# Order of the TensorE products inside a split step and inside a differential head

## The chip, the cores and the metric

The kernel runs on one core of a Trainium2 chip. The metric is the device time of one execution in microseconds (us), the median of several executions; before the change it is 1139.26 us (three executions, 1139.25 to 1139.76).

## The reference, cut to what matters

One layer of a hybrid decoder on x of 256 tokens by 2048 columns, all in float32. One input projection of the normalised x (2048 columns wide) gives six blocks of 1024 columns; the first three feed eight differential heads, the last three eight stick-breaking heads. An output projection and a squared-ReLU MLP of 8192 hidden columns follow, each added to the residual, and a last RMSNorm.

```python
h = rmsnorm(x, ln1[l])
dq, dk, dv, sq, sk, sv = jnp.split(h @ w_in[l], split_points, axis=-1)
# differential head: two softmax maps over 64 dims each, values of 128 dims
w = probs(q1, k1) - lam * probs(q2, k2)
o = jnp.einsum("bhqk,bkhd->bqhd", w, v)
...
x = x + mixed @ w_out[l]
h = rmsnorm(x, ln2[l])
x = x + jnp.square(jax.nn.relu(h @ w_mlp_in[l])) @ w_mlp_out[l]
```

## The kernel before

**Numbers in two parts.** Every long product is made of three products of float32r operands. A matrix is split into H, its float32r rounding, and L, the rest; x.w is taken as xH.wH + xH.wL + xL.wH, summed in float32 in PSUM. The weights stream from HBM in chunks of 512 rows by 512 columns (1 MB, three buffers). ScalarE casts half a chunk to `wh` (L214) and VectorE subtracts to get `wl` (L217); such a half, 256 contraction rows by 512 columns, is a split step. Four pairs of `wh` and `wl` are in flight (six in the MLP), and the casts run three to five steps ahead of the products.

**Two forms of product.** `products_acc` (L248) keeps the activations in the array and moves the weights: three products of 512 columns for each contraction tile and token tile (L258 to L260). It serves dq, dk, dv, sv, the output projection (`oacc`) and the second MLP product (`ma`). `products_T` (L264) keeps the weights in the array and moves the activations. It serves sq and sk (`acc_sq`, `acc_sk`) and the first MLP product (`ia`). For one contraction tile and one tile of 128 weight columns it issues a long product, `wh` against H and L of the activations side by side (512 columns, L272), and a short one, `wl` against H alone (256 columns, L274), which is added to the second half of the same PSUM bank. A step of `products_T` has four column tiles times two contraction tiles, so eight long and eight short products. A group is the eight steps (2048 contraction rows) that fill four banks. In its last step each column tile is evacuated by `done(i)` as soon as its own products are out: ScalarE copies the second half of the bank, VectorE adds the first half to it (L568 for sq and sk).

**A differential head.** `diff_task` (L441) computes both score maps of a head into one tile `sc` of two PSUM banks, map m in bank m. A map has a 64-dim query and key: map 0 lies in partitions 0 to 63 of `qT` and `kT`, map 1 in partitions 64 to 127. For each map there is a mask product of 128 rows in bf16 (identity times mask, L451), a score product of query tile 1 against 256 keys (L453) and one of query tile 0 against 128 keys (L455). These two are plain float32, and the profile records each of them as two instructions. The attention tasks are generators that are advanced between the split steps; their instructions stand on the same TensorE queue as the products of the weight stream.

**Order.** Outside of the first seven steps, which are written out by hand, a scheduler with a timeline model of its own orders the instructions of an engine; it keeps to the program's order, except that it may put a ready instruction ahead of one that waits in its model.

Of the kernel before, what the change touches and what calls it, by code (L numbers as in the profile page):

```python
# [10 lines left out]
F32 = mybir.dt.float32  # L11
F32R = mybir.dt.float32r
BF16 = mybir.dt.bfloat16
# [3 lines left out]
PSUM = bass.MemoryType.PSUM  # L17

P = 128
S = 256  # L20
D = 2048
DFF = 4 * D
NT = S // P          # token tiles
KT = D // P          # contraction tiles of the model width
NB = 512             # columns of a weight block
CK = 4               # contraction tiles of one weight load
HK = 2               # contraction tiles of one split step
HG = 4               # heads of one column block
# [5 lines left out]
LN_IN = 2.0 ** -32                    # the Ln table ends at 2^64  # L34
LN_OUT = -16.0 * math.log(2.0)
LAM_INIT = 0.8 - 0.6 * math.exp(-0.3 * 0)
W_BUFS = 3           # weight loads in flight
S_BUFS = 4           # split steps in flight
START_ORDER = "x0 c0 x1 c1 m0 x2 c2 m1 c3 x3 m2 x4 c4 m3 c5 x5 m4 x6 c6 m5 c7 x7 m6"
WARM0, WARM1 = 5, 4  # products of zeros before and after the first transposes  # L40
AHEAD = 3            # split steps ahead of the products
# [3 lines left out]
def tile_hybrid_layer(  # L45
# [19 lines left out]
    """Every large product runs as three float32r passes: with x = H + L, H = float32r(x),  # L65
    x.w = xH.wH + xH.wL + xL.wH, all summed in float32 PSUM."""
# [9 lines left out]
    # ---------------------------------------------------------------- loads  # L76
# [16 lines left out]
    # ---------------------------------------------------------------- constants  # L93
# [14 lines left out]
    negtri = cpool.tile([P, P], F32, name="negtri")      # [l, j] = -1 where l >= j  # L108
# [5 lines left out]
    dmask = cpool.tile([P, 2 * P], BF16, name="dmask")   # [q, key]: key <= q is kept  # L114
    smask = cpool.tile([P, 2 * P], BF16, name="smask")   # [key, q]: key < q is kept
# [12 lines left out]
    # ---------------------------------------------------------------- helpers  # L128
    def rsqrt_mean(ss, n, width, name, r, eps=EPS, most=FMAX):
        """r = 1 / sqrt(ss / width + eps): exp(-ln/2), then one Newton step; 0 where the sum of  # L130
        squares exceeds `most` (it overflows, and the root of its inverse is 0)."""
        v = tiny.tile([P, n], F32, tag=f"v{n}", name=f"v_{name}")
        nc.vector.tensor_scalar(v, ss, 1.0 / width, eps, op0=ALU.mult, op1=ALU.add)
        nc.vector.tensor_scalar(v, v, TINY, BIG, op0=ALU.max, op1=ALU.min)
        lv = tiny.tile([P, n], F32, tag=f"lv{n}", name=f"lv_{name}")
        nc.scalar.activation(lv, v, AF.Ln, scale=LN_IN)
        r0 = tiny.tile([P, n], F32, tag=f"r0{n}", name=f"r0_{name}")
        nc.scalar.activation(r0, lv, AF.Exp, scale=-0.5, bias=lnout_c)
        a = tiny.tile([P, n], F32, tag=f"a{n}", name=f"a_{name}")
        nc.vector.scalar_tensor_tensor(a, v, -0.5, r0, op0=ALU.mult, op1=ALU.mult)  # L140
        nc.vector.tensor_tensor(a, a, r0, op=ALU.mult)
        nc.vector.scalar_tensor_tensor(a, a, 1.5, r0, op0=ALU.add, op1=ALU.mult)
        nc.vector.scalar_tensor_tensor(r, ss, most, a, op0=ALU.is_le, op1=ALU.mult)

    def split_pair(dst, ps, g, per_kt):
        """dst[:, kt, 0/1, :] = H / L of ps * g (g: one column per kt, or one for both)."""
        if per_kt:
            for j in range(HK):
                nc.scalar.activation(dst[:, j, 0, :], ps[:, j * S:(j + 1) * S], AF.Copy, scale=g[:, j:j + 1])
            for j in range(HK):  # L150
                nc.vector.scalar_tensor_tensor(dst[:, j, 1, :], ps[:, j * S:(j + 1) * S], g[:, j:j + 1],
                                               dst[:, j, 0, :].bitcast(F32),
                                               op0=ALU.mult, op1=ALU.subtract)
        else:
            pv = ps.rearrange("p (k s) -> p k s", k=HK)
            nc.scalar.activation(dst[:, :, 0, :], pv, AF.Copy, scale=g)
            nc.vector.scalar_tensor_tensor(dst[:, :, 1, :], pv, g,
                                           dst[:, :, 0, :].bitcast(F32),
                                           op0=ALU.mult, op1=ALU.subtract)

    # ---------------------------------------------------------------- weight stream
    jobs = []       # (chunk id, half, products, after)
    chunks = []     # weight views
# [10 lines left out]
    mlp = {"n": 0}  # pools of the second part  # L174
# [72 lines left out]
    # activations stationary, weights moving: acc[t] += act[:, tokens t].T @ w  # L247
# [15 lines left out]
    # weights stationary, activations moving: acc[i] = [wH.T @ xH | wH.T @ xL + wL.T @ xH]  # L263
    def products_T(get_acc, act, k0, done):  # L264
        def f(h, wh, wl):
            acc = get_acc()
            for i in range(NB // P):
                fs = slice(i * P, (i + 1) * P)
                for j in range(HK):
                    kt = k0 + h * HK + j  # L270
                    a = act(kt)
                    nc.tensor.matmul(acc[i], wh[:, j, fs], a.rearrange("p a s -> p (a s)"),  # L272
                                     start=kt == 0, stop=False, skip_group_check=True)
                    state["mm"] = nc.tensor.matmul(acc[i][:, S:2 * S], wl[:, j, fs], a[:, 0, :],  # L274
                                                   start=False, stop=kt == KT - 1, skip_group_check=True)
                if kt == KT - 1:
                    done(i)
        return f
# [17 lines left out]
    # ---------------------------------------------------------------- start: x -> xs  # L296
# [9 lines left out]
    def keep_clock_up(n, name):  # L306
        """products of zeros that nothing reads: the tensor engine's clock is halved until it
        has been busy for a while, and it has to wait for the first loads anyway."""
# [5 lines left out]
    lamc = cpool.tile([P, 2], F32, name="lamc")          # c, -lam * c with c = 1 / max(|lam|, 1)  # L314
    epsc = cpool.tile([P, 1], F32, name="epsc")          # eps * c^2
    mostc = cpool.tile([P, 1], F32, name="mostc")        # float32's largest value * c^2
# [72 lines left out]
    # ---------------------------------------------------------------- attention tasks  # L389
    grp = {}  # L390

    def prep_task(kind):
        """q / k of the differential heads: rotary, then heads transposed to [dim, token]."""
# [28 lines left out]
    def finish_pair(o, g, kt2, name, **norm):  # L422
        """per-head RMSNorm of o [q, (head, query tile), dim], transposed and split into mixT."""
# [17 lines left out]
    def diff_task(gi):  # L441
        while f"dk{gi}" not in grp:
            yield
        # outputs carry the factor c, so that their squares stay in range for any lam
        qT, kT, v = grp[f"dq{gi}"], grp[f"dk{gi}"], grp[f"dv{gi}", "src"]
        for h in range(HG):
            nm = f"d{gi}{h}"
            sc = ps_sc.tile([P, 2, 512], F32, tag="sc", name=f"sc_{nm}")
            for m in range(2):
                dm = slice(m * 64, (m + 1) * 64)  # L450
                nc.tensor.matmul(sc[:, m, P:3 * P], identb, dmask, start=True, stop=False,  # L451
                                 skip_group_check=True)
                nc.tensor.matmul(sc[:, m, 0:S], qT[dm, h, P:S], kT[dm, h, 0:S],  # L453
                                 start=False, stop=False, skip_group_check=True)
                nc.tensor.matmul(sc[:, m, S:S + P], qT[dm, h, 0:P], kT[dm, h, 0:P],  # L455
                                 start=False, stop=True, skip_group_check=True)
            yield
            nm4 = tiny.tile([P, 2, 2], F32, tag="nmax", name=f"nmax_{nm}")   # [query tile, map]
# [40 lines left out]
    def sb_task(gi):  # L499
        """scores as [key, query]: columns are (key tile 0, query tile 1), (0, 0), (1, 1)."""  # L500
# [47 lines left out]
    # ---------------------------------------------------------------- projections  # L548
# [3 lines left out]
    def proj_T_block(kind):  # L552
        """q / k of the stick-breaking heads, straight to [dim, token]."""
# [58 lines left out]
    # output projection: the first two column blocks stop before the last head group  # L612
# [50 lines left out]
    # ---------------------------------------------------------------- MLP stream  # L663
# [12 lines left out]
    FQ = 4                       # quarters of the hidden width  # L676
    FG = DFF // FQ // NB         # column groups of a quarter
# [34 lines left out]
    def out_group(q, nb):  # L712
# [29 lines left out]
        # the last column block: all of token tile 0, then token tile 1 in two column halves  # L742
# [55 lines left out]
    def square_base(t, n):  # L798
        """the sum over all but the last piece, ready before it."""
# [4 lines left out]
    def finish_tokens(t, base):  # L804
        """final RMSNorm of one token tile; all but the last column block are times ln_f already."""
# [38 lines left out]
    # ---------------------------------------------------------------- run  # L844
# [31 lines left out]
def _rope_table():  # L876
    """cos | cos and -sin | sin of the first 16 dims, [token in tile, token tile, 2, 16]."""
# [36 lines left out]
```

## Time and profile before

| | |
|---|---|
| median of three executions | 1139.26 us |
| span of the profiled execution, first to last instruction | 1137.4 us |
| what lies around the span (1139.26 less 1137.4) | 1.9 us |
| TensorE (PE) busy | 1126.2 us, 99% of the span |
| weight loads (PEld) | 948.9 us, 83% |
| VectorE (DVE) busy | 659.2 us, 58% |
| ScalarE (ACT) busy | 534.6 us, 47% |
| HBM traffic over the span | 182 GB/s |

The span is the profiled execution's own time inside the program; the sum of a change is made against it, and what lies around it is taken as constant. Ends of TensorE instructions in the records are modelled, so the time that a product costs is read from the start of one to the start of the next, not from its duration. PEld rows are the loads of the stationary operand; they run beside the products.

### The profile page before, as it was taken

The numbers are of one execution on the slowest core, as the hardware profiler recorded it, in microseconds if no ns is written. First come the engines' busy times: TensorE is split into PE (matmuls) and PEld (weight loads), VectorE is DVE, ScalarE is ACT, GpSimd is POOL, SyncE is SP. The second block draws the span as 40 slices with busy tenths as digits, with TensorE's granted clock in tenths as the row PEclk, the third lists the DMA queues.
The fourth block names the chain that finished last, engine by engine and source line by source line (L and its number), as shares of the span: only waits on it lengthen the run. The fifth ranks groups of instructions, "written<-read, shape, count | busy, mean of one in ns | idle before, by whom it ended". The sixth has DMA issues, their size and how long they took to land.

```text
span 1137.4 us, 14314 instructions
## 1 busy us (share of the span) xinstructions
PE 1126.2 (99%) x5725; PEld 948.9 (83%) x5725; DVE 659.2 (58%) x929; ACT 534.6 (47%) x761; POOL 2.9 (0%) x16
## 2 busy tenths in 40 slices
PE   9999999999999999999999999999999999999996
PEld 6887888888888888888888888888888888888886
DVE  5755656656655656565455556455655545565652
ACT  5644444555554644453334444334544333454531
POOL 1000000000000000000000000000000000000000
PEclk9999999999999999999999999999999999999998
DMA  8744454444555855555565555556555566555502
GB/s 289 231 153 157 148 179 146 149 148 148 184 187 199 322 182 185 185 186 193 197 199 186 186 185 185 192 194 196 189 192 185 185 190 191 191 190 195 193 35 74
DMA packets 105207, 207.68 MB, mean 183 GB/s; under 512 B 4114, under 2 KB 5172, under 8 KB 105012
## 3 DMA queue, kind: packets, MB, share of 16 engines
q1 hardware_dynamic: 104852, 206.24, 55.0%
q8 instruction: 45, 0.74, 0.3%
q10 hardware_dynamic: 288, 0.52, 0.1%
q14 instruction: 22, 0.18, 0.0%
HBM read 204.65 MB, written 2.10 MB: 182 GB/s over the span
## 4 chain that ended last, share of the span: by engine, by line
PE 97%; DMA 2%; SPq 1%; DVE 0%; ACT 0%; issue 0%; DVEq 0%; ACTq 0%
PE ia L272 21%; PE ia L274 11%; PE ma L260 10%; PE ma L259 10%; PE ma L258 10%; PE acc_sk L272 3%; PE acc_sq L272 3%; PE oacc L260 3%; PE oacc L258 3%; PE oacc L259 3%; PE acc_sq L274 1%; PE acc_sk L274 1%; PE acc_dk L258 1%; PE acc_dk L260 1%; PE acc_sv L258 1%; PE acc_dk L259 1%
## 5 line engine op out<-in xcount | busy, mean ns | idle before, releaser
L217 DVE TENSOR_TENSOR wl<-w,wh 128x1024 fp32r<-128x1024 f32 (+1 forms) x385 | 469.1, 1222 | 396.7 <-ACT wh L214 394.8
L214 ACT CAST wh<-w 128x1024 fp32r<-128x1024 f32 (+1 forms) x385 | 401.8, 1048 | 485.3 <-PE ma L260 189.7
L272 PE MATMUL ia<-xs,wh 128*128 128x512 f32 x1024 | 357.4, 393 | 0.0
L274 PE MATMUL ia<-xs,wl 128*128 128x256 f32 x1024 | 285.7, 281 | 0.0
L272 PEld LDWEIGHTS ia<-xs,wh 128*128 128x128 f32 x1024 | 191.1, 187 | 43.0
L274 PEld LDWEIGHTS ia<-xs,wl 128*128 128x128 f32 x1024 | 193.0, 189 | 1.2
L260 PE MATMUL ma<-wh,aT 128*128 128x512 f32 x480 | 187.9, 391 | 0.0
L259 PE MATMUL ma<-wl,aT 128*128 128x512 f32 x480 | 187.8, 391 | 0.0
L258 PE MATMUL ma<-wh,aT 128*128 128x512 f32 x480 | 187.7, 391 | 0.0
L258 PEld LDWEIGHTS ma<-wh,aT 128*128 128x128 f32 x480 | 90.1, 188 | 19.9
L259 PEld LDWEIGHTS ma<-wl,aT 128*128 128x128 f32 x480 | 90.1, 188 | 19.8
L260 PEld LDWEIGHTS ma<-wh,aT 128*128 128x128 f32 x480 | 90.1, 188 | 19.8
L258 PE MATMUL oacc<-wh,mixT 128*128 128x512 f32 x128 | 50.6, 395 | 0.0
L259 PE MATMUL oacc<-wl,mixT 128*128 128x512 f32 x128 | 50.2, 392 | 0.0
L260 PE MATMUL oacc<-wh,mixT 128*128 128x512 f32 x128 | 49.9, 394 | 0.0
L272 PE MATMUL acc_sq<-xs,wh 128*128 128x512 f32 x128 | 45.3, 396 | 0.0
L272 PE MATMUL acc_sk<-xs,wh 128*128 128x512 f32 x128 | 44.9, 398 | 0.0
L274 PE MATMUL acc_sq<-xs,wl 128*128 128x256 f32 x128 | 35.8, 284 | 0.0
L274 PE MATMUL acc_sk<-xs,wl 128*128 128x256 f32 x128 | 34.4, 283 | 0.0
L260 PEld LDWEIGHTS oacc<-wh,mixT 128*128 128x128 f32 x128 | 24.0, 188 | 5.0
L258 PEld LDWEIGHTS oacc<-wh,mixT 128*128 128x128 f32 x128 | 24.1, 188 | 4.9
L259 PEld LDWEIGHTS oacc<-wl,mixT 128*128 128x128 f32 x128 | 24.1, 188 | 4.9
(225 smaller groups left out, 1128.5 us busy)
## 6 DMA issues: line engine op xcount, KB each, us to landing
w<-in_w_mlp_in_dram SPq DMA_DIRECT2D x64, 1024.0 KB, 5.4
w<-in_w_mlp_out_dram SPq DMA_DIRECT2D x64, 1024.0 KB, 5.0
w<-in_w_in_dram SPq DMA_DIRECT2D x46, 1024.0 KB, 5.2
w<-in_w_out_dram SPq DMA_DIRECT2D x16, 1024.0 KB, 5.1
w<-in_w_in_dram SPq DMA_DIRECT2D x4, 512.0 KB, 7.7
x<-in_x_dram SPq DMA_DIRECT2D x3, 512.0 KB, 10.3
lnf_t<-in_ln_f_dram SPq DMA_DIRECT2D x1, 1024.0 KB, 6.5
out_dram<-x SPq DMA_DIRECT2D x4, 256.0 KB, 3.0
```

What stands on the lines that cost most here:

```text
L214: state["wh"] = nc.scalar.copy(wh[:, j], w[:, j])
L217: state["wl"] = nc.vector.tensor_tensor(wl[:, j], w[:, j], wh[:, j].bitcast(F32), op=ALU.subtract)
L258: nc.tensor.matmul(acc[t], a[:, 0, st], wh[:, j, :], start=s0, stop=False)
L259: nc.tensor.matmul(acc[t], a[:, 0, st], wl[:, j, :], start=False, stop=False)
L260: state["mm"] = nc.tensor.matmul(acc[t], a[:, 1, st], wh[:, j, :], start=False, stop=s1)
L272: nc.tensor.matmul(acc[i], wh[:, j, fs], a.rearrange("p a s -> p (a s)"), start=kt == 0, stop=False, skip_group_check=True)
L274: state["mm"] = nc.tensor.matmul(acc[i][:, S:2 * S], wl[:, j, fs], a[:, 0, :], start=False, stop=kt == KT - 1, skip_group_check=True)
```

## The change

There are two edits (the rest of the diff takes comments away).

In `products_T` the order of a step's 16 products changes. Before, long and short alternated for each column tile and contraction tile. Now all eight long products of a step come first and then its eight short ones. In the last step of a group, where each column tile is evacuated as soon as it is complete, the order is two long and two short for each column tile.

In `diff_task` the two mask products come first, then L453's product of map 0 and of map 1, then L455's product of map 0 and of map 1. Before, map 0 was completed before map 1 began. No product is added or left out by either edit.

```diff
     def products_T(get_acc, act, k0, done):
         def f(h, wh, wl):
             acc = get_acc()
-            for i in range(NB // P):
-                fs = slice(i * P, (i + 1) * P)
-                for j in range(HK):
-                    kt = k0 + h * HK + j
-                    a = act(kt)
-                    nc.tensor.matmul(acc[i], wh[:, j, fs], a.rearrange("p a s -> p (a s)"),
-                                     start=kt == 0, stop=False, skip_group_check=True)
-                    state["mm"] = nc.tensor.matmul(acc[i][:, S:2 * S], wl[:, j, fs], a[:, 0, :],
-                                                   start=False, stop=kt == KT - 1, skip_group_check=True)
-                if kt == KT - 1:
-                    done(i)
+            last = k0 + (h + 1) * HK == KT
+
+            def high(i, j):
+                kt = k0 + h * HK + j
+                nc.tensor.matmul(acc[i], wh[:, j, i * P:(i + 1) * P], act(kt).rearrange("p a s -> p (a s)"),
+                                 start=kt == 0, stop=False, skip_group_check=True)
+
+            def low(i, j):
+                kt = k0 + h * HK + j
+                state["mm"] = nc.tensor.matmul(acc[i][:, S:2 * S], wl[:, j, i * P:(i + 1) * P], act(kt)[:, 0, :],
+                                               start=False, stop=kt == KT - 1, skip_group_check=True)
+
+
+            tiles = range(NB // P)
+            for part in ([(i,) for i in tiles] if last else [tiles]):
+                for one in (high, low):
+                    for i in part:
+                        for j in range(HK):
+                            one(i, j)
+                if last:
+                    done(part[0])
         return f
...
             sc = ps_sc.tile([P, 2, 512], F32, tag="sc", name=f"sc_{nm}")
+
             for m in range(2):
-                dm = slice(m * 64, (m + 1) * 64)
                 nc.tensor.matmul(sc[:, m, P:3 * P], identb, dmask, start=True, stop=False,
                                  skip_group_check=True)
-                nc.tensor.matmul(sc[:, m, 0:S], qT[dm, h, P:S], kT[dm, h, 0:S],
-                                 start=False, stop=False, skip_group_check=True)
-                nc.tensor.matmul(sc[:, m, S:S + P], qT[dm, h, 0:P], kT[dm, h, 0:P],
-                                 start=False, stop=True, skip_group_check=True)
+            for cs, qs, ks, last in ((slice(0, S), slice(P, S), slice(0, S), False),
+                                     (slice(S, S + P), slice(0, P), slice(0, P), True)):
+                for m in range(2):
+                    dm = slice(m * 64, (m + 1) * 64)
+                    nc.tensor.matmul(sc[:, m, cs], qT[dm, h, qs], kT[dm, h, ks],
+                                     start=False, stop=last, skip_group_check=True)
             yield
```

## Rows read from the trace of the kernel before

**Rows 1.** The page: busy time of TensorE, and its granted clock in 40 slices.

```profile
PE 1126.2 (99%) x5725; PEld 948.9 (83%) x5725; DVE 659.2 (58%) x929; ACT 534.6 (47%) x761; POOL 2.9 (0%) x16
...
PEclk9999999999999999999999999999999999999998
```

**Rows 2.** Waits of TensorE, the longest of three: us in total, times, longest.

```profile
PE warm_a L311 <- DVE three_c L105: 1.3, 1, 1.3
```

**Rows 3.** Groups of instructions by line, TensorE: count, busy us, mean ns, idle before.

```profile
L272 PE MATMUL ia<-xs,wh 128*128 128x512 f32 x1024 | 357.4, 393 | 0.0
L274 PE MATMUL ia<-xs,wl 128*128 128x256 f32 x1024 | 285.7, 281 | 0.0
...
L272 PE MATMUL acc_sq<-xs,wh 128*128 128x512 f32 x128 | 45.3, 396 | 0.0
...
L453 PE MATMUL sc_d<-T_dk,T_dq 64*128 64x256 f32 x32 | 11.1, 428 | 0.0
...
L455 PE MATMUL sc_d<-T_dk,T_dq 64*128 64x128 f32 x32 | 6.3, 277 | 0.0
...
L451 PE MATMUL sc_d<-dmask,identb 128*128 128x256 bf16 x16 | 4.5, 282 | 0.0
```

**Rows 4.** Timeline of TensorE in the first MLP product: start us, us, instruction.

```profile
630.11 0.39 PE L272 MATMUL ia<-xs,wh 128*128 128x512 f32 x1
630.34 0.28 PE L274 MATMUL ia<-xs,wl 128*128 128x256 f32 x1
...
635.31 0.40 PE L272 MATMUL ia<-xs,wh 128*128 128x512 f32 x1
```

**Rows 5.** Timeline of TensorE in the second MLP product: long rows, then short rows.

```profile
1107.73 0.39 PE L752 MATMUL ma<-wl,aT 128*128 128x512 f32 x1
...
1111.58 0.40 PE L751 MATMUL ma<-wh,aT 128*128 128x512 f32 x1
...
1117.10 0.28 PE L751 MATMUL ma<-wh,aT 128*128 128x256 f32 x1
...
1122.81 0.28 PE L751 MATMUL ma_last<-wh,aT 128*128 128x256 f32 x1
```

**Rows 6.** Timeline of TensorE over the scores of one differential head.

```profile
111.62 0.28 PE L451 MATMUL sc_d<-dmask,identb 128*128 128x256 bf16 x1
111.84 0.70 PE L453 MATMUL sc_d<-T_dk,T_dq 64*128 64x256 f32 x2
112.37 0.38 PE L455 MATMUL sc_d<-T_dk,T_dq 64*128 64x128 f32 x2
112.69 0.28 PE L451 MATMUL sc_d<-dmask,identb 128*128 128x256 bf16 x1
...
113.75 0.50 PE L258 MATMUL acc_dk<-wh,xs 128*128 128x512 f32 x1
114.08 0.40 PE L259 MATMUL acc_dk<-wl,xs 128*128 128x512 f32 x1
```

**Rows 7.** Timeline, single instructions of the first head's map 0.

```profile
80.05 0.48 PE L453 MATMUL sc_d<-T_dk,T_dq 64*128 64x256 f32 x1
...
80.37 0.38 PE L453 MATMUL sc_d<-T_dk,T_dq 64*128 64x256 f32 x1
...
80.70 0.27 PE L455 MATMUL sc_d<-T_dk,T_dq 64*128 64x128 f32 x1
...
80.90 0.28 PE L451 MATMUL sc_d<-dmask,identb 128*128 128x256 bf16 x1
```

**Rows 8.** Timeline of TensorE, mask product of a stick-breaking head.

```profile
258.21 0.27 PE L509 MATMUL sc_s<-smask,identb 128*128 128x256 bf16 x1
258.32 0.83 PE L512 MATMUL sc_s<-T_sq,T_sk 128*128 128x128 f32 x6
```

**Rows 9.** Timeline where acc_sq gives its banks to acc_sk.

```profile
271.73 0.39 PE L272 MATMUL acc_sk<-xs,wh 128*128 128x512 f32 x1
...
275.42 0.42 DVE L568 TENSOR_TENSOR t_sq<-acc_sq,t_sq 128x256 f32<-128x256 f32 x1 [0.49 <-ACT t_sq L567]
```

## The prediction

> **What bounds the kernel now.** I read the page first. [...] A busy TensorE proves little by itself, since the ends of its records are modelled, so the second view was its waits: it waited three times in the whole execution, never longer than 1.3 us, and all of it in the start [rows 2]. From there to the last column block no product waits for a cast, a transfer or a bank. The kernel is therefore as long as the sum of the slots that its products take, a slot being the time from one start to the next. Whatever shortens a slot shortens the kernel, and no other engine's work is in the way as long as it keeps up, which it did with VectorE at 58% and ScalarE at 47% [rows 1].
>
> The third view, the groups of instructions, says how many slots the change touches: 1024 pairs of a long and a short product in the first MLP product, 128 in `acc_sq`, and the same again in `acc_sk`, so 1280 pairs; and in the differential heads 16 masks, 32 instructions of L453 and 32 of L455 [rows 3]. That is eight heads of two maps, with each float32 product recorded as two instructions. Their durations are of no use here (393 and 281 ns overlap each other), so the last view was the timeline, for slots.
>
> **Edit one: long products first.** Now a pair takes 15 pairs / 5.20 us: from 630.11 to 635.31 there are 15 long ones, each with its short one, so 347 ns a pair; the first long slot is 0.23 us, which leaves 0.12 for the short [rows 4]. After the change long follows long and short follows short. The trace has both, in the second MLP product. Seventeen slots of 512 columns take 1111.58 - 1107.73 = 3.85 us, 226.5 ns each, and 48 slots of 256 columns take 1122.81 - 1117.10 = 5.71 us, 119.0 ns each [rows 5]. Those are the same sizes and types with a new stationary operand each time, and they add to the same bank several times in a row. Long plus short is then 345.5 ns instead of 346.7, 1.2 ns less. Seven of eight steps of a group are regrouped as blocks of eight, where seven of eight neighbours are alike; in the last step only one neighbour in two is. So 0.83 of the pairs gain: 1280 x 0.83 x 1.2 ns = 1.3 us gained.
>
> The bounds: slots are read to 10 ns at both ends of a stretch, so 20 ns over 15 pairs is 1.3 ns a pair, as large as the difference. From this the edit lies between nothing and twice as much, 0 to 2.6 us gained. I take 1.3. Apart from the slots the edit moves waits. The first `wl` of a step is needed eight long slots later (1.8 us), which can only help; its last `wh` is read about 0.8 us earlier, which frees a buffer sooner. Against it, the fourth bank of a group is written six long slots into the first step (1.4 us) instead of six pairs (2.1 us). The tightest place is sq to sk, where all four banks are taken over at once: `acc_sk` starts at 271.73, and the last bank of `acc_sq` is only read out by the add of 275.42, 3.7 us later [rows 9]. TensorE didn't wait there even so [rows 2], because the scheduler puts products of the tiles that are already free in front. Since even 2.1 us were less than 3.7, this cover does the work today and I cost the shift of 0.7 us at nothing. If the cover were gone, two such hand-overs times 0.7 us, 1.4 us, would be lost.
>
> **Edit two: the two maps alternate.** Now a head takes from 111.62 to 113.75, 2.13 us, or 1.07 for a map: mask 0.22, L453 0.53, L455 0.32 [rows 6]. Much of it is no product. The same mask of 256 columns in front of products of 128 rows takes 0.11 [rows 8]; in front of L453, of 64 rows, 0.22, so entering the 64-row products costs 0.11. The first instruction of L453 takes 0.32 until the second starts, and its record is 0.10 longer than the second's (0.48 against 0.38) [rows 7]; the second takes 0.53 - 0.32 = 0.21, so 0.11 is a load of the stationary operand that nothing covers. The second instruction of L455 holds the queue from 80.70 to 80.90, 0.20 [rows 7], while the two together take 0.32 [rows 6], so the first has 0.12 and 0.08 to 0.09 is spent on leaving. Together a visit to the 64-row products costs 0.11 + 0.11 + 0.09 = 0.31 us beside its work, of 4 instructions: 2 x 0.215 + 2 x 0.11 = 0.65. A head makes two visits now and would make one.
>
> That alone gives, for a head after the change: two masks 0.22, entry and load 0.22, eight instructions 4 x 0.215 + 4 x 0.11 = 1.30, exit 0.09, in all 1.83 instead of 2.13. So 0.30 x 8 heads = 2.4 us.
>
> The other half depends on what happens when an instruction of map 0 (partitions 0 to 63) is followed by one of map 1 (64 to 127) that writes another bank. No two such neighbours stand in the trace; a mask lies between the maps [rows 6]. One bound is full overlap: the array works on both halves of its rows at once. Starts stay in order, so the second instruction of L453 for map 0 runs beside the first for map 1, the second for map 1 beside L455's first and second for map 0, and L455's two for map 1 come last: 3 x 0.215 + 2 x 0.11 = 0.865 instead of 1.30, 0.435 less. The head is 1.395, a saving of 0.735 x 8 = 5.9 us. The other bound is that each change of half costs a whole visit, 0.31. There are three changes (to map 1, back for L455, to map 1 again), 0.93, against the 0.31 saved: 0.62 x 8 = 5.0 us lost.
>
> I take the overlap. [...]
>
> [...]
>
> **The sum.** Against the profiled execution: 1137.4 - 1.3 - 5.9 = 1130.2 us of span. 1139.26 - 1137.4 = 1.9 us lie around the span and stay, which gives 1132.1 us against the median. A difference under 0.2%, 2.3 us, is about what a measurement of this kernel can't tell from no change.
>
> **The rivals.**
> 1. *One visit instead of two, but no overlap.* For it: every neighbour in the heads now runs one after the other, and float32 products come as two instructions. Against it: the disjoint rows. 1139.26 - 1.3 - 2.4 = 1135.6 us.
> 2. *The second edit does nothing.* A change of half costs one uncovered load, 0.11, as at L453's first instruction [rows 7]. Three of them are 0.33, which eats the 0.30. What is left is the first edit: 1139.26 - 1.3 = 1138.0, or no change at all if the 1.2 ns are an error of reading.
> 3. *Slower: a change of half is a full exit and entry.* 1139.26 - 1.3 + 5.0 = 1143.0 us. It breaks even where three changes cost 0.31 + 1.3 / 8 = 0.47 us, so 0.16 each, and it is slower by over 0.2% from (0.47 + 2.3 / 8) / 3 = 0.25 us each. For it: an entry with its load costs 0.22 and an exit 0.09 wherever the rows show them [rows 6, 7]. Against it: those are between 128 and 64 rows, not between halves.
>
> **How the numbers follow.** Overlap 0.52 (1130.8 to 1133.4, the bounds of edit one), one visit without overlap 0.25 (1134.3 to 1136.9), nothing from edit two 0.15 (1136.7 to 1139.3), a full exit at each change 0.08. The likeliest gives 1132.1. The range reaches from 1130.5 into rival 2, to 1138.1, which leaves out the upper half of rival 2 and rival 3, some 0.16, and a little below. Faster by over 0.2% means under 1137.0: the overlap, rival 1 and a little of rival 2, 0.78. Within 0.2%: 0.14. Slower: 0.08.
>
> **What would show it.** In the MLP's first product eight starts 0.227 us apart and then eight 0.119 apart; pairs that average 347 ns or more refute edit one. In a head, the masks 0.11 apart, and L453's first instruction of map 1 within some 10 ns of map 0's second if they overlap; 0.21 later means rival 1, 0.32 rival 2, over 0.4 rival 3. A head should take 1.4 us from first mask to the next product. The waits of TensorE should stay at those of the start; a row with `acc_sk` waiting for VectorE would be the lost cover. The forecast is wrong if the scheduler pulls the pieces of a head apart, so that a head makes more visits than one, or if the start order of halves costs what rival 2 or 3 says.

## The result and the profile after

The changed kernel takes 1132.84 us (median of 4 executions, 1131.97 to 1134.03) against 1139.51 us of the kernel before on the same chips (1139.25 to 1140.45): ratio 0.9939, 95% interval 0.9925 to 0.9953. That is 6.7 us or 0.6% faster. The profiled execution took 1131.97 us with a span of 1130.3, 7.1 us shorter than the span of before.

The page of the changed kernel answers to [rows 1]: TensorE is as full as it was (99% of the span), and its clock as high (mean granted clock 0.998, before 0.997).

```profile
span 1130.3 us, 14306 instructions
...
PE 1119.3 (99%) x5725; PEld 945.4 (84%) x5725; DVE 662.8 (59%) x929; ACT 536.8 (47%) x761; POOL 2.9 (0%) x16
...
PEclk9999999999999999999999999999999999999999
```

Its waits answer to [rows 2]: still three, all in the start, none longer than 1.3 us. So neither edit brought a new wait, and the 7.1 us came out of the slots.

```profile
PE warm_a L321 <- DVE three_c L105: 1.3, 1, 1.3
PE ps_g1T L309 <- DMA rows<-in_ln_dram: 0.5, 1, 0.5
PE xtp L344 <- DMA x<-in_x_dram: 0.4, 1, 0.4
```

Where they came out of is read from the first start of two groups. Each row ends with minimum, median and maximum duration, the first and last start, and the forms. First the kernel before, then the changed one: the masks of the differential heads and the long products of the MLP's first product.

```profile
L451 PE MATMUL sc_d<-dmask,identb x16: 273/283/286, 79.8 to 196.6; 128*128 128x256 bf16 x16
L272 PE MATMUL ia<-xs,wh x1024: 387/391/487, 417.4 to 1039.8; 128*128 128x512 f32 x171
```

```profile
L461 PE MATMUL sc_d<-dmask,identb x16: 272/273/283, 79.6 to 191.4; 128*128 128x256 bf16 x16
L271 PE MATMUL ia<-xs,wh x1024: 387/393/482, 409.9 to 1032.5; 128*128 128x512 f32 x171
```

From the first head's mask to the first MLP product it was 417.4 - 79.8 = 337.6 us and is 409.9 - 79.6 = 330.3: 7.3 us gone in the stage that holds the heads. From there to the last long MLP product it was 622.4 us and is 622.6: nothing gained where 1024 of the 1280 pairs lie.

A head, to be set beside [rows 6]: the timeline of TensorE in the changed kernel.

```profile
79.62 0.39 PE L461 MATMUL sc_d<-dmask,identb 128*128 128x256 bf16 x2
79.94 0.92 PE L467 MATMUL sc_d<-T_dk,T_dq 64*128 64x256 f32 x8
80.80 0.50 PE L258 MATMUL acc_dq<-wh,xs 128*128 128x512 f32 x1
81.13 0.40 PE L259 MATMUL acc_dq<-wl,xs 128*128 128x512 f32 x1
```

Both masks stand together, then all eight 64-row instructions in one visit, and the next product comes 80.80 - 79.62 = 1.18 us after the first mask; it was 2.13. The overlap is seen in narrow windows of the same timeline, whose merged rows count the instructions that have started. A window that ends at 79.948 holds one of them, the next, to 80.00, holds two:

```profile
79.94 0.48 PE L467 MATMUL sc_d<-T_dk,T_dq 64*128 64x256 f32 x1
79.94 0.49 PE L467 MATMUL sc_d<-T_dk,T_dq 64*128 64x256 f32 x2
```

Two records start within 0.01 us of each other and together span 0.49, where the first alone has 0.48. The load records of the same two windows show the loads of the two maps side by side too, the first alone with 0.18 us, both together with 0.19:

```profile
79.94 0.18 PEld L467 LDWEIGHTS sc_d<-T_dk,T_dq 64*128 64x128 f32 x1 [0.21 <-issue]
79.94 0.19 PEld L467 LDWEIGHTS sc_d<-T_dk,T_dq 64*128 64x128 f32 x2 [0.21 <-issue]
```

The first MLP product, to be set beside [rows 4], in the changed kernel:

```profile
621.96 2.00 PE L271 MATMUL ia<-xs,wh 128*128 128x512 f32 x8
623.80 1.11 PE L276 MATMUL ia<-xs,wl 128*128 128x256 f32 x8
624.75 2.00 PE L271 MATMUL ia<-xs,wh 128*128 128x512 f32 x8
```

Eight long slots take 623.80 - 621.96 = 1.84 us, 230 ns each, and eight short ones 0.95 us, 118.8 each: in this stretch the pair is 348.8 ns and not 345.5.

### The profile page after: what moved, and what is told of

Read it like the earlier page. It is cut to its first block, busy times and chain, and to the rows that moved or that the text cites. A ratio compares the mean times of both kernels' runs of the same rounds, so it can differ in the third digit from the quotient of the medians.

```text
span 1130.3 us, 14306 instructions
## 1 busy us (share of the span) xinstructions
PE 1119.3 (99%) x5725; PEld 945.4 (84%) x5725; DVE 662.8 (59%) x929; ACT 536.8 (47%) x761; POOL 2.9 (0%) x16
## 4 chain that ended last, share of the span: by engine, by line
PE 99%; DMA 0%; DVE 0%; SPq 0%; ACT 0%; issue 0%; DVEq 0%; ACTq 0%
PE ia L271 21%; PE ia L276 11%; PE ma L260 10%; PE ma L259 10%; PE ma L258 10%; PE acc_sk L271 3%; PE acc_sq L271 3%; PE oacc L260 3%; PE oacc L258 3%; PE oacc L259 3%; PE acc_dq L258 1%; PE acc_sq L276 1%; PE acc_sk L276 1%; PE acc_dk L258 1%; PE acc_dk L260 1%; PE acc_dq L260 1%
## 5 line engine op out<-in xcount | busy, mean ns | idle before, releaser
L271 PE MATMUL ia<-xs,wh 128*128 128x512 f32 x1024 | 267.7, 393 | 0.0
L271 PEld LDWEIGHTS ia<-xs,wh 128*128 128x128 f32 x1024 | 180.0, 189 | 28.4
L276 PEld LDWEIGHTS ia<-xs,wl 128*128 128x128 f32 x1024 | 147.8, 189 | 15.8
L276 PE MATMUL ia<-xs,wl 128*128 128x256 f32 x1024 | 152.2, 282 | 0.0
L271 PE MATMUL acc_sk<-xs,wh 128*128 128x512 f32 x128 | 36.7, 399 | 0.0
L271 PE MATMUL acc_sq<-xs,wh 128*128 128x512 f32 x128 | 34.9, 397 | 0.0
L712 ACT COPY t<-ia 128x256 f32<-128x256 f32 x64 | 23.8, 372 | 20.0 <-PE ia L276 20.0
L714 DVE TENSOR_TENSOR s<-ia,t 128x256 f32<-128x256 f32 x64 | 26.9, 420 | 1.9
```

The lines of the kernel that those rows point to most:

```text
L271: nc.tensor.matmul(acc[i], wh[:, j, i * P:(i + 1) * P], act(kt).rearrange("p a s -> p (a s)"), start=kt == 0, stop=False, skip_group_check ...
L712: nc.scalar.copy(t1, acc[i][:, S:2 * S])
L714: nc.vector.tensor_tensor(s, acc[i][:, 0:S], t1, op=ALU.add)
```

## The experiments

All were run with the kernel before on the same chip. Besides the ratios, two figures of each trace are used, because they repeat far better than a time: the stretch from the first mask to the first MLP product ("head stage"), and TensorE's busy time in the first MLP product, summed over its four groups.

| kernel | ratio, 95% interval | head stage, us | first MLP product, PE us |
|---|---|---|---|
| before | 1 | 337.6 | 359.12 |
| the change | 0.9939 (0.9925 to 0.9953) | 330.3 | 359.56 |
| heads_only | 0.9937 (0.9925 to 0.9950) | 330.7 | 359.12 |
| steps_only | 1.0002 (0.9993 to 1.0011) | 337.4 | 359.56 |
| same_half | 0.9984 (0.9975 to 0.9993) | 335.4 | 359.12 |
| map_by_map | 0.9943 (0.9930 to 0.9957) | 330.7 | 359.12 |
| steps_j_outer | 0.9936 (0.9923 to 0.9950) | 330.2 | 359.56 |
| heads_whole | 0.9936 (0.9923 to 0.9948) | 330.7 | 359.12 |
| moving_weights | 0.9930, one execution | 330.3 | 358.80 |
| stationary_acts | 0.9940, one execution | 330.8 | 359.25 |

**heads_only: the heads' new order without that of the steps.** `products_T` is that of the kernel before.

> The differential heads' new order alone; the long and short products of a split step alternate as before. Theory (the heads carry the whole gain, because a whole float32 product of map 1 runs beside the whole product of map 0, not only its neighbouring half): 7.2 to 7.7 us under the kernel before, so a ratio near 0.9935, as fast as the full change or up to 0.5 us faster; a head takes 1.17 us from the first mask to the next product. Rival (the split of the prediction: heads 5.9, steps 1.3): 5.9 us under the kernel before, ratio 0.9948, slower than the full change by 1.3 us.

Measured 1132.43 us against 1139.5, ratio 0.9937 (0.9925 to 0.9950), and a head of 1.18 us. The heads carry the gain. The head stage shrank by 6.9 us, nearer to the theory's 7.2 than to the prediction's 5.9. The ratio's interval alone, 5.7 to 8.5 us, would hold both.

**steps_only: the steps' new order without that of the heads.** `diff_task` is that of the kernel before.

> The new order of the long and short products alone; the heads as before. Theory: nothing, or up to 0.7 us slower (the four groups of the first MLP product took 0.1 us longer each under the full change), ratio 1.000 to 1.0006. Rival (the prediction): 1.3 us faster, ratio 0.9989.

Measured 1139.64 us against 1139.5, ratio 1.0002 (0.9993 to 1.0011). No change that can be measured; the expected 1.3 us lie just beyond the interval's lower end, which is 0.8 us. The trace says it more sharply. TensorE's busy time in the four groups of the first MLP product, the last line of the view by stretches, kernel before and then steps_only:

```profile
sum 364.00, PE 359.12 PEld 313.93 DVE 21.85 ACT 22.10; mean PE 89.78 PEld 78.48 DVE 5.46 ACT 5.53
```

```profile
sum 363.50, PE 359.56 PEld 314.58 DVE 24.55 ACT 22.31; mean PE 89.89 PEld 78.65 DVE 6.14 ACT 5.58
```

The sum before it is only the width of the stretches; PE is what counts. It is 0.44 us longer with the new order, 0.4 ns for each of 1024 pairs, and the same 359.56 comes back in the changed kernel, while heads_only and the other kernels with the old order of the steps show the 359.12 of before to the hundredth. In the head stage the new order wins about as much back, 0.2 us here and 0.4 between heads_only and the change.

**same_half: one visit, but no second half to overlap with.** On top of heads_only:

```diff
-                    dm = slice(m * 64, (m + 1) * 64)
+                    dm = slice(0, 64)
```

> As heads_only, but map 1 of every head reads map 0's query and key (partitions 0 to 63), so that both maps are the same map and all four products of a head use the same half of the rows; this changes what is computed. One visit to the 64-row products is left, overlap is impossible. Theory (overlap is worth 0.65 us a head, the saved visit 0.30): a head takes 1.83 us, 2.4 us under the kernel before, ratio 0.998. Rival (the saved visit and the masks side by side carry most of it): a head stays near 1.2 us and the ratio near 0.9935.

Measured 1137.67 us against 1139.5, ratio 0.9984 (0.9975 to 0.9993), 0.8 to 2.9 us. The timeline of the first head:

```profile
80.07 0.39 PE L450 MATMUL sc_d<-dmask,identb 128*128 128x256 bf16 x2
80.39 1.57 PE L456 MATMUL sc_d<-T_dk,T_dq 64*128 64x256 f32 x8
81.89 0.50 PE L258 MATMUL acc_dq<-wh,xs 128*128 128x512 f32 x1
```

A head takes 81.89 - 80.07 = 1.82 us, and the eight instructions that took 0.86 in the changed kernel (79.94 to 80.80) take 1.50. So of the 0.95 us that a head gained, 0.31 belong to the saved visit and 0.64 to the overlap.

**map_by_map: masks first, but each map's two products together.** On top of the kernel before:

```diff
             for m in range(2):
-                dm = slice(m * 64, (m + 1) * 64)
                 nc.tensor.matmul(sc[:, m, P:3 * P], identb, dmask, start=True, stop=False,
                                  skip_group_check=True)
+            for m in range(2):
+                dm = slice(m * 64, (m + 1) * 64)
                 nc.tensor.matmul(sc[:, m, 0:S], qT[dm, h, P:S], kT[dm, h, 0:S],
                                  start=False, stop=False, skip_group_check=True)
                 nc.tensor.matmul(sc[:, m, S:S + P], qT[dm, h, 0:P], kT[dm, h, 0:P],
                                  start=False, stop=True, skip_group_check=True)
```

> Masks of both maps first, then both products of map 0, then both of map 1: one visit, but only the short product of map 0 stands beside the long one of map 1. Theory (products start in the order of the queue, and one waits only for its own half): a head takes 1.6 to 1.7 us, 3.4 to 4.2 us under the kernel before, ratio 0.9963 to 0.9970. Rival (the engine takes a ready product of the other half ahead of the queue): the head takes 1.17 us as in the full change, ratio 0.9935.

The theory fell here. Measured 1132.84 us against 1139.5, ratio 0.9943 (0.9930 to 0.9957); the head takes 83.05 - 81.86 = 1.19 us as in the full change. On TensorE's queue, the compiled order of the first head is this, the first two lines of map 0 and the last two of map 1:

```
L454 MATMUL sc_d_808<-T_dk_674,T_dq_510 128x256
L456 MATMUL sc_d_808<-T_dk_674,T_dq_510 128x128
L454 MATMUL sc_d_808<-T_dk_674,T_dq_510 128x256
L456 MATMUL sc_d_808<-T_dk_674,T_dq_510 128x128
```

and the trace has this, all four L454 records (both maps' long products, two records each) ahead of any of L456:

```profile
81.86 0.39 PE L450 MATMUL sc_d<-dmask,identb 128*128 128x256 bf16 x2
82.19 0.71 PE L454 MATMUL sc_d<-T_dk,T_dq 64*128 64x256 f32 x4
82.72 0.40 PE L456 MATMUL sc_d<-T_dk,T_dq 64*128 64x128 f32 x4
83.05 0.50 PE L258 MATMUL acc_dq<-wh,xs 128*128 128x512 f32 x1
```

The long product of map 1 started with that of map 0 (two records from 82.19 on that together span 0.49 us), past the short product of map 0 that stood ahead of it on the queue (L456, from 82.72 on). The alternation of the maps in the program isn't what the gain needs. It needs the mask of map 1 out from between the maps: 2.13 us a head with it there, 1.19 without.

**steps_j_outer: another order within the long products.** On top of the full change:

```diff
-                    for i in part:
-                        for j in range(HK):
+                    for j in range(HK):
+                        for i in part:
                             one(i, j)
```

> The heads' new order together with long products first, but with the contraction tile in the outer loop: consecutive long products share the moving operand and each goes to another bank; with the changed kernel two in a row share the bank and the moving operand changes every time. Theory (a long slot of this form costs 231 ns whoever is its neighbour): as heads_only, 7 us under the kernel before, ratio 0.9937, long slots near 231. Rival (two products in a row to one bank, or the change of the moving operand, cost the 4 ns by which the slot missed the 227 of the other form): long slots near 227 and some 4 us less than heads_only (1280 pairs x 0.83 x 4 ns), ratio near 0.990.

Measured 1132.61 us against 1139.99, ratio 0.9936 (0.9923 to 0.9950), and again 359.56 us in the first MLP product. Bank and moving operand of the neighbour made no difference: the rival is out.

**heads_whole: no head torn apart.** In both kernels the scheduler pulls the second head apart with transposes of the head before. In the kernel before this head took 93.42 - 90.28 = 3.14 us, from its first mask to the next product:

```profile
90.28 0.28 PE L451 MATMUL sc_d<-dmask,identb 128*128 128x256 bf16 x1
...
93.42 0.50 PE L258 MATMUL acc_dq<-wh,xs 128*128 128x512 f32 x1
```

In the changed kernel it takes 2.61 us, from 89.12 to 91.73, with two more returns to the 64-row products and overlap in only part of them:

```profile
89.12 0.39 PE L461 MATMUL sc_d<-dmask,identb 128*128 128x256 bf16 x2
89.44 0.70 PE L467 MATMUL sc_d<-T_dk,T_dq 64*128 64x256 f32 x2
90.06 0.44 PE L493 MATMUL wtp_d<-ident,e_d 128*128 128x128 f32 x2
90.43 0.70 PE L467 MATMUL sc_d<-T_dk,T_dq 64*128 64x256 f32 x4
91.06 0.33 PE L493 MATMUL wtp_d<-ident,e_d 128*128 128x128 f32 x1
91.32 0.48 PE L467 MATMUL sc_d<-T_dk,T_dq 64*128 64x128 f32 x2
91.73 0.50 PE L258 MATMUL acc_dq<-wh,xs 128*128 128x512 f32 x1
```

On top of heads_only, the masks and score products are queued behind those transposes:

```diff
-                nc.tensor.transpose(tp[:, i * P:(i + 1) * P], w[:, i * P:(i + 1) * P], ident)
+                state["wtp"] = nc.tensor.transpose(tp[:, i * P:(i + 1) * P], w[:, i * P:(i + 1) * P], ident)
...
+            with ExitStack() as st:
+                if "wtp" in state:
+                    st.enter_context(tc.issue_after(state["wtp"].ins))
...
```

> heads_only, and a head's score products are queued behind the transposes of the head before, so that no head is torn apart by them. Theory: the torn second head makes three visits to the 64-row products and takes 2.6 us with 0.7 us of transposes in it; whole it takes 1.17, so some 0.8 to 1.1 us less than heads_only, ratio near 0.993, if the later start of some heads makes nothing else wait. Rival (the waits of the attention chain show once heads start later): no gain or a loss, with a new row among the waits of TensorE.

The rival held. The second head is whole, but the ratio is 0.9936 (0.9923 to 0.9948), the head stage 330.7 us as in heads_only, and there is a new row among the waits, of the size of the gain:

```profile
PE wtp_d L485 <- DVE e_d L480: 0.9, 1, 0.9
```

**moving_weights and stationary_acts: which operand makes the long slot long.** Each replaces one operand of the long product in the changed kernel. First moving_weights, then stationary_acts:

```diff
-                nc.tensor.matmul(acc[i], wh[:, j, i * P:(i + 1) * P], act(kt).rearrange("p a s -> p (a s)"),
+                act(kt)
+                nc.tensor.matmul(acc[i], wh[:, j, i * P:(i + 1) * P], wl[:, j, :],
```

```diff
-                nc.tensor.matmul(acc[i], wh[:, j, i * P:(i + 1) * P], act(kt).rearrange("p a s -> p (a s)"),
+                nc.tensor.matmul(acc[i], act(kt)[:, 0, 0:P], act(kt).rearrange("p a s -> p (a s)"),
```

> The full change, with the long product of a pair moving 512 columns of the step's low weights through the array instead of the activations (the stationary operand stays the high weights); this changes what is computed. Mean long slot of the first MLP product, 231.5 ns in the changed kernel, 229.1 in the second MLP product, which moves weights. Theory (the difference comes from the moving activations): 229 ns, and the four groups of the first MLP product together some 1.5 to 2.5 us shorter. Rival (it comes from the stationary weights): 231.5 still, group lengths as in the changed kernel.

> The full change, with the long product's stationary operand taken from the activations instead of the high weights (the moving operand stays the activations); this changes what is computed. Theory (the moving activations make the difference): long slot 231.5 ns still. Rival (the stationary weights make it): 229 ns, and the four groups of the first MLP product together some 1.5 to 2.5 us shorter.

Both ran once, in 1131.47 and 1132.61 us against 1139.45. The first MLP product took 358.80 us with weights moving and 359.25 with activations stationary, against 359.56. That is 0.8 and 0.3 us, and neither is the 1.5 to 2.5 that was expected of the operand that makes the difference. Neither operand alone makes the difference.

## Why the prediction was right

**What bounds the kernel** held: with no new wait, every slot saved became time saved, 7.1 us of span against 7.2 predicted. The sum, 1130.2 us of span and 1132.1 of time, met 1130.3 and 1132.84 (1131.97 in the execution that was profiled). That they met so closely is luck: two terms were off in opposite directions, by about 1 us each.

**Edit one was mis-sized: 1.3 us gained in the text, nothing measured** (steps_only, ratio 1.0002). The step that failed is "Long plus short is then 345.5 ns instead of 346.7". Both figures come from short stretches. Over the whole stage a pair takes 359.12 / 1024 = 350.7 ns before and 359.56 / 1024 = 351.1 after, which refutes the edit by the prediction's own sign, 347 ns or more. The short slots came as forecast, 118.8 ns against 119.0. The long ones came at 231.5 in the mean where the text took 226.5 [rows 5]. Of these 5.0 ns, 2.6 are the choice of the stretch, since the mean of the whole second MLP product is 229.1; the other 2.4 lie between the two forms of product. And the order changes the long slot little: in the traces' starts its mean is 231.8 ns before, with a short product behind each, and 231.5 after. The text named nothing gained as a bound, and that is where it ended. That the shift of banks costs nothing held: no row with `acc_sk` or `ia` waiting appeared. One reading was off without effect: a step's first `wl` stood behind one long product already, so it is needed seven long slots later, 1.6 us, and not eight.

**Edit two had the overlap right and the order of starts within it wrong, so its size was too small: 5.9 us in the text, 6.9 in the head stage of heads_only.** Entry, uncovered load and exit were right: same_half, which has one visit and no overlap, was forecast at 1.83 us a head and took 1.82. The step that failed is "Starts stay in order, so the second instruction of L453 for map 0 runs beside the first for map 1". No run shows that order: in the changed kernel the records of both maps start within 0.01 us of each other at 79.94, loads included, and in map_by_map L454 of the second map started at 82.19, ahead of the first L456, at 82.72. The eight instructions take 0.86 us with the exit and the first load in it, instead of 0.11 + 0.865 + 0.09 = 1.07; that is the time of one map alone, 0.11 + 0.65 + 0.09 = 0.85. The head is 1.18 us instead of 1.395, and 0.95 is saved instead of 0.735. Over eight heads that would be 7.6, but the torn second head saves only 3.14 - 2.61 = 0.53, with the same three transposes in both; 7 x 0.95 + 0.53 = 7.2, and 6.9 to 7.3 were measured.

That the maps overlap at all was the author's estimate, since no row of before has a product of one map next to one of the other. The changed kernel shows it by the two records that span 0.49 us, and same_half by its 1.50 us for the eight instructions that take 0.86 when each map has its own half.

**The rivals.** One visit without overlap would have been 1135.6 us; same_half shows what that looks like, 1137.67 us without edit one. A load or a full exit at each change of half, rivals 2 and 3, didn't occur: the starts of the two maps lie 0.01 us apart. That the scheduler might pull a head apart was named as a danger; it happened to one head of eight, as in the kernel before (in the fifth head a mask runs 13 us ahead in both kernels, which tears no score products apart), and mending it (heads_whole) only turned the gain into a wait.

**What stays open:** why the long slot with stationary weights takes 231.5 ns in the mean and that with stationary activations 229.1, and why it varies within one product. The neighbour's bank and moving operand are excluded (steps_j_outer); replacing one operand took away 0.3 or 0.8 us, where 2.4 ns over 1024 long slots would be 2.5. Nor is it shown why the new order loses 0.4 us in the MLP and wins about as much before it, or whether the two maps would overlap in one bank, which no run tried.

## What to carry to other kernels

Where products contract over 64 rows, put those of different halves of the partitions next to each other, in different banks as here, with nothing of 128 rows in between: here the second half's products cost almost no time of their own (eight instructions in 0.86 us, one map alone 0.85 by the estimate above), and the return to 64-row products that was saved gave another 0.31 us a head. The order among them mattered little (a head of 1.18 or 1.19 us); what stood between them mattered (2.13 us with a mask there), so masks, transposes and pieces that a scheduler slips in are to be looked for first. And a slot that is to be borrowed from another stage has to be of the same form, and averaged over the whole stage rather than a clean stretch: the stretch put the long slot off by 2.6 ns and the form by 2.4, each twice the forecast gain of 1.2 ns a pair.

## What the runs showed of the hardware

TensorE took a product of the other row half past one that stood before it on its queue (map_by_map, L454 of map 1 from 82.19 us on, L456 of map 0 from 82.72), and the 64-row float32 products of two maps, each recorded as two instructions, ran side by side: eight instructions in 0.86 us, against 1.50 when all used the same half, and an estimated 0.85 for one map alone. A span of busy time over one stage repeats to 0.01 us between runs of different kernels (359.12 in five, 359.56 in three), while whole executions of one kernel differ by some 2 us (1131.97 to 1134.03). In the traces shown the spread lies ahead of the heads: the first mask starts at 79.62 us in the changed kernel and at 81.86 in map_by_map, whose profiled execution took 1134.35 us and whose head stage is only 0.4 us longer. So effects of 0.4 us in 1130 can be read from a trace where no timing shows them.
